# A hybrid decoder layer: SiLU by its own activation, decays computed one supertile ahead, two PSUM banks for the chunk products

## The chip, the cores and the metric

The kernel runs on one core of a Trainium2 chip. The metric is the device time of one execution in microseconds (us). The engines are TensorE (PE in the profile; its weight loads are PEld), VectorE (DVE), ScalarE (ACT), GpSimd (POOL), and the DMA queue that SyncE (SP) issues to.

## The reference

One layer over a prompt of 4096 tokens, 1024 wide, and 8 sample tokens. `h = x * (1 + scale) + shift` is projected by `w_in`. Head group A is a gated delta rule on 4 heads of 128; head group B is attention in a window of 128 with sinks. Both are gated, joined, projected by `w_out` and normalised. What the change touches:

```python
qkv = silu(causal_conv(h @ w_in[:, :1536], conv_w))      # 4 taps per channel
q, k = l2_normalize(qa) * 128**-0.5, l2_normalize(ka)
beta = sigmoid(...)
g = -exp(a_log) * softplus(... + dt_bias)                # decay, per token and head
G = cumsum(g)                                            # within a chunk
dec = exp(G[t] - G[i]) for t >= i
lower = I + beta * (k @ k.T) * dec                       # inverted per chunk
a_qk = (q @ k.T) * dec
```

## The kernel before, in words

The work has three stages. Stage one walks over 16 supertiles of 256 tokens, two chunks of 128 each, and does head group A. Stage two walks over 32 tiles of 128 tokens and does the window attention. Stage three does the gates `z`, the output projection and the normalisation for 16 pairs of tiles. The sample tokens are worked in between as side tasks.

One supertile of stage one goes through `front(s, ...)` (from line 260), `lanes` (line 405), `gdn_inv` (line 440) and `gdn_c` (line 485):

- Lines 262 to 284 project 8 columns of beta and decay (`bd`, from `wbd` and `hT`), and form `be` and `g16`. The softplus is `softplus_ops` (line 96): one `Exp` on ACT (`spu`, line 101) and a polynomial of ten small DVE instructions in a row (lines 103 to 106).
- `group` (line 296) is called for keys, queries and values (blocks 4 to 7, 0 to 3, 8 to 11 of the projection). Each makes two pairs of blocks, 48 matmuls of 128x256 a pair into `pj`; ACT copies (lines 309, 313), DVE adds three taps a block (line 315). Then the gate: ACT's `Tanh` into `th` (line 321) and one DVE instruction `(th + 1) * dst` (line 322), which leaves twice the SiLU.
- Lines 329 to 350 make the decays: the running sum `G` by two matmuls from `g16` (into `tr`), its `Exp` (line 333), and for each chunk a bank `pga` of matmuls, four `Exp` into `dec` (line 348) and one into `eGl` (line 349).
- Lines 352 to 359 transpose the keys of a chunk into `tr`; ACT squares them and scales them with `dec` to `Kd`.
- Lines 370 to 382 make the products keys by keys and keys by queries in bank `pga`, two heads at a time; DVE turns them into `U` and `Aqk`. `lanes` starts the inverse of `U` with 62 small DVE instructions (lines 421, 423) between trips through DRAM.

PSUM has eight banks here: `pga` 1, `xt` 1 (side tasks), `tr` 1 (transposes), `pj` 2, `pgi` 3.

The order on each engine is not that of the source. The framework's scheduler puts the instructions of all engines in order ahead of time, by its own costs and by program order as priority, and fills gaps on TensorE with projection matmuls of a neighbouring supertile. Each engine then works its list strictly in that order and waits where an operand is late.

`dec_b1` (line 914) is the sample tokens' attention; it loads keys, values and sinks for 8 samples with 24 transfers. `loadS` (line 1008) fetches the 7 MB weights `wz` and `wo` of stage three, each in one transfer.

Of the kernel before, what the change touches and what calls it, by code (L numbers as in the profile page):

```python
# [9 lines left out]
F32 = mybir.dt.float32  # L10
F16 = mybir.dt.float16
# [6 lines left out]
D = 1024  # L18
OFF_AZ = 1536
# [14 lines left out]
def body(ctx, tc, I, O, seq):  # L34
# [76 lines left out]
    with ExitStack() as p1:  # L111
# [7 lines left out]
        pga = p1.enter_context(tc.tile_pool(name="pga", bufs=1, space=PSUM))  # L119
        pxt = p1.enter_context(tc.tile_pool(name="pxt", bufs=1, space=PSUM))  # L120
# [139 lines left out]
        def front(s, hT, ahead):  # L260
# [11 lines left out]
            be = sml.tile([128, 2, 4], F32, name="be")  # L272
# [8 lines left out]
            g16 = sml.tile([128, 2, 8], F16, name="g16")  # L281
            gf = g.rearrange("p a b -> p (a b)")
            dve.tensor_copy(g16[:, 0], gf)
            dve.tensor_sub(g16[:, 1], gf, g16[:, 0])
            kqv = wk.tile([128, 8, 256], F32, name="kqv", bufs=2)
# [7 lines left out]
            sc = sml.tile([128, 6, 8], F32, name="sc")  # L293
# [35 lines left out]
            ps = tr_ps([128, 8])  # L329
            mm(ps, triU, g16[:, 0], True, False)  # L330
            mm(ps, triU, g16[:, 1], False, True)
            G = sml.tile([128, 4, 8], F32, name="G")
            act.activation(G[:, 0], ps, AF.Exp)
            act.activation(G[:, 1], ps, AF.Copy, scale=-1.0)
            dve.tensor_scalar(G[:, 2], G[:, 0], -1.0, None, op0=ALU.mult)
            eGl = sml.tile([128, 2, 4], F32, name="eGl")
            decs = []
            for c in range(2):
                dec = wf.tile([128, 4, 128], F32, name="dec", bufs=2)
                pg = pga.tile([128, 4, 128], F32, name="pga")  # L340
                for h in range(4):
                    m = 4 * c + h
                    mm(pg[:, h, :], idb, negm, True, False)
                    mm(pg[:, h, :], g16[:, 0, m:m + 1].to_broadcast([128, 128]), triU, False, False)
                    mm(pg[:, h, :], g16[:, 1, m:m + 1].to_broadcast([128, 128]), triU, False, True)
                for h in range(4):
                    m = 4 * c + h
                    act.activation(dec[:, h, :], pg[:, h, :], AF.Exp, bias=G[:, 1, m:m + 1])
                act.activation(eGl[:, c, :], pg[:, :, 127], AF.Exp)
                decs.append(dec)  # L350

# [8 lines left out]
            dve.tensor_scalar(sse[:, 1], sse[:, 1], 4e-6, None, op0=ALU.add)  # L360
            dve.tensor_scalar(sc[:, 5], sse[:, 1], 0.25, None, op0=ALU.mult)
            pool.tensor_tensor(sc[:, 0], sc[:, 5], half_pos[:, 0:8], op=ALU.pow)
# [30 lines left out]
            dve.tensor_scalar(sc[:, 4], sse[:, 0], 4e-6, 1.28e-4, op0=ALU.add, op1=ALU.mult)  # L393
# [307 lines left out]
        load_bd()  # L701
        for g in (4, 5, 6, 7):
            split_w1(g, wst[g - 4])
# [5 lines left out]
        def ahead(s):  # L709
            if s < NS:  # L710
                nxt[0] = xt(s, load_x(s))

        for s in range(NS):
            kqv, G, sc, U16, Aqk, Kd, Vn, eGl, vt, vt16 = front(s, nxt[0], lambda: ahead(s + 1))
# [25 lines left out]
    with ExitStack() as p2:  # L740
# [173 lines left out]
        def dec_b1(T):  # L914
            sp.dma_start(O["swa_k_s"][0, :, 0:127], I["cache_swa_k"][0, :, 1:128])
            sp.dma_start(O["swa_v_s"][0, :, 0:127], I["cache_swa_v"][0, :, 1:128])
            ps = tr_ps([128, 6, 16])
# [43 lines left out]
            Vc = T.tile([128, 8, 128], F32, name="eVc")  # L961
            for b in range(8):
                kT = T.tile([128, 129], F32, name="ekT", bufs=2)
                sp.dma_start(kT[:, 0:128], I["ckT"][b])
                sp.dma_start(Vc[:, b, :], I["cache_swa_v"][0, b].rearrange("t a d -> t (a d)"))
                dve.tensor_copy(kT[:, 128:129], kn[:, b:b + 1])
                mm(ps_s, Qz[:, b * 64:(b + 1) * 64], kT, b == 0, b == 7)
            sk = T.tile([64, 1], F32, name="esk")
            for b in range(8):
                sp.dma_start(sk[8 * b:8 * b + 8, :], I["sinks"].rearrange("o h -> h o"))  # L970
# [37 lines left out]
        def loadS(w, blk):  # L1008
            sp.dma_start(w.rearrange("p r q a k c -> p r (q a k c)"), wS[blk].rearrange("r p x -> p r x"))
# [278 lines left out]
        for i in range(NT):  # L1288
# [7 lines left out]
            if i == 2:  # L1296
                loadS(wz, 0)
# [22 lines left out]
        loadS(wo, 1)  # L1320
# [74 lines left out]
def layouts(a):  # L1395
# [9 lines left out]
    def chan(v):  # L1405
# [23 lines left out]
        "ckT": a["cache_swa_k"][0].reshape(8, 128, 128).transpose(0, 2, 1),  # L1429
# [27 lines left out]
```

## Time and profile before

| | us |
|---|---|
| median of 3 runs (2236.66 to 2239.43) | 2238.08 |
| the profiled execution | 2235.32 |
| its span, first to last instruction | 2233.5 |
| TensorE busy in the span | 2098.6 (94%) |
| VectorE busy | 1831.9 (82%) |
| ScalarE busy | 1269.1 (57%) |
| mean granted TensorE clock, share of full speed | 0.982 |

The profile is of one execution; line numbers are those of the kernel above. "Busy" is the time that an engine spends on instructions. A wait is idle time of an engine just before an instruction, put down to the event that came last before it started. Stage one ends at about 1100 us, stage two at about 1570 us.

### The profile page before, as it was taken

How to read it: one execution, taken by the hardware profiler on the slowest of the kernel's cores; microseconds unless marked ns; L12 is line 12 of the kernel's file. 1: busy time of each engine (PE TensorE's matmuls, PEld its weight loads, DVE VectorE, ACT ScalarE, POOL GpSimd, SP SyncE). 2: the span in 40 equal slices, each digit the busy share in tenths (PEclk: the TensorE clock that was granted, in tenths of full speed). 3: DMA queues.
4: the chain of work that ended last, by engine and by line, in shares of the span. 5: the costliest groups of instructions: out<-in, count | busy, mean ns of one | idle time of the engine just before them, and what ended most of it. 6: DMA issues, size and time to landing. Idle time of an engine off the chain costs nothing.

```text
span 2233.5 us, 48900 instructions
## 1 busy us (share of the span) xinstructions
PE 2098.6 (94%) x18287; PEld 1497.6 (67%) x18287; DVE 1831.9 (82%) x5546; ACT 1269.1 (57%) x3601; POOL 163.4 (7%) x284
## 2 busy tenths in 40 slices
PE   6989999999989999898999999999999999999997
PEld 4877888878778888777676777776445545444443
DVE  7778889888889989888878977776786787888877
ACT  6666877666767776655446666666443333334332
POOL 1101111111111111011000000000000000000000
PEclk9999999999999999999999999999998999999999
DMA  8333332332233332213153111110532333323222
GB/s 331 105 114 92 130 91 93 119 105 68 88 98 107 107 115 81 67 51 114 54 215 119 59 60 60 61 58 23 222 100 91 131 114 114 117 87 132 95 98 72
DMA packets 141679, 232.21 MB, mean 104 GB/s; under 512 B 62852, under 2 KB 75448, under 8 KB 135272
## 3 DMA queue, kind: packets, MB, share of 16 engines
q1 hardware_dynamic: 140144, 228.53, 30.1%
q8 instruction: 144, 2.36, 0.4%
q14 instruction: 95, 0.78, 0.1%
q10 hardware_dynamic: 1296, 0.55, 0.1%
HBM read 154.07 MB, written 76.09 MB: 103 GB/s over the span
## 4 chain that ended last, share of the span: by engine, by line
PE 53%; DVE 28%; ACT 11%; DMA 4%; issue 3%; POOL 0%; POOLq 0%; SPq 0%; ACTq 0%; DVEq 0%
PE pp L1042 21%; PE pj L41 11%; PE pgi L41 6%; DVE kqv L315 5%; DVE lt L421 3%; PE pga L41 3%; ACT Sm L872 3%; DVE LV L423 3%; PE po L41 2%; PE tr L41 2%; PE tr L889 2%; DMA x<-in_xT_dram 1%; DVE kqv L322 1%; PE xt L41 1%; PE pS L41 1%
## 5 line engine op out<-in xcount | busy, mean ns | idle before, releaser
L41 PE MATMUL pj<-hT,w 128*128 128x256 f16 x4608 | 575.7, 275 | 3.4 <-ACT hT L255 2.6
L41 PEld LDWEIGHTS <-w 128*128 128x128 f16 x4800 | 450.0, 99 | 65.1 <-issue 11.4
L1042 PEld LDWEIGHTS <-S 128*128 128x128 f16 x1536 | 150.6, 99 | 171.4 <-issue 5.0
L41 PEld LDWEIGHTS <-hT 128*128 128x128 f16 x2048 | 159.8, 98 | 68.8 <-issue 4.1
L41 PE MATMUL pj<-wq,hT 128*128 128x512 f16 x768 | 194.8, 379 | 1.1 <-DVE qt L783 0.6
L315 DVE SCALAR_TENSOR_TENSOR kqv<-u,cols,kqv 128x256 f32<-128x256 f32 x384 | 181.9, 480 | 3.7 <-ACT kqv L313 3.1
L1042 PE MATMUL pp<-wz,S 128*128 128x512 f16 x768 | 182.1, 383 | 0.0
L1042 PE MATMUL pp<-wo,S 128*128 128x512 f16 x768 | 171.3, 379 | 0.7 <-DVE zs L1218 0.6
L872 ACT ACTIVATE Sm<-Sm,nm 128x256 f32<-128x256 f32 (+1 forms) x256 | 125.5, 492 | 56.0 <-DVE nm L869 56.0
L1042 PE MATMUL pp<-wz,hT 128*128 128x512 f16 x576 | 131.9, 380 | 1.2 <-ACT zs L1129 1.2
L421 DVE TENSOR_TENSOR lt<-LV,LU 128x60 f32<-128x60 f32 (+24 forms) x496 | 120.2, 242 | 5.8
L1042 PE MATMUL pp<-wo,A 128*128 128x512 f16 x540 | 122.1, 379 | 0.0
L865 DVE CUSTOM_DVE_ANT_0 Sm<-pS,swam 128x256 f32<-128x256 f32 (+1 forms) x256 | 96.2, 415 | 28.2 <-PE tr L889 27.3
L423 DVE TENSOR_TENSOR LV<-LV,lt 128x60 f32<-128x60 f32 (+24 forms) x496 | 103.4, 208 | 5.8
L1042 PEld LDWEIGHTS <-hT 128*128 128x128 f16 x612 | 59.8, 98 | 71.8 <-issue 2.8
L41 PE MATMUL pj<-wkv,hT 128*128 128x256 f16 x768 | 105.6, 273 | 0.0
L1081 POOL TENSOR_TENSOR rs<-rs,cf 128x1 f32<-128x1 f32 (+1 forms) x33 | 22.8, 692 | 1070.7 <-DVE rs L1080 1070.7
L41 PE MATMUL pga<-kqv 128*128 128x256 f32 x256 | 72.2, 401 | 24.2 <-DVE kqv L322 24.1
L1042 PEld LDWEIGHTS <-A 128*128 128x128 f16 x540 | 52.8, 99 | 62.0
L1023 ACT ACTIVATE S<-zt 128x512 f16<-128x512 f32 x64 | 40.3, 630 | 85.7 <-DVE zt L1029 81.4
L1136 ACT ACTIVATE zs<-zs 128x512 f32<-128x512 f32 x48 | 30.2, 629 | 101.3 <-DVE zs L1135 101.2
L315 DVE SCALAR_TENSOR_TENSOR vv<-u,cols,vv 128x256 f32<-128x256 f32 x192 | 82.3, 479 | 1.7 <-ACT vv L313 1.0
(378 smaller groups left out, 4574.7 us busy)
## 6 DMA issues: line engine op xcount, KB each, us to landing
hT<-hD SPq DMA_DIRECT2D x32, 1024.0 KB
x<-in_xT_dram SPq DMA_DIRECT2D x32, 512.0 KB
hD<-hT SPq DMA_DIRECT2D x16, 1024.0 KB
x<-in_x_prompt_dram SPq DMA_DIRECT2D x60, 256.0 KB
out_y_prompt_dram<-x SPq DMA_DIRECT2D x60, 256.0 KB
stg<-in_ws_dram SPq DMA_DIRECT2D x16, 512.0 KB
LU<-D SPq DMA_DIRECT2D x64, 128.0 KB
wS<-wt SPq DMA_DIRECT2D x16, 512.0 KB
```

The lines of the kernel that those rows point to most:

```text
L41: pe.matmul(out, l, r, start=st, stop=sp_)
L315: dve.scalar_tensor_tensor(d, u[:, b2, j:j + 256], cwj(j, blk), d, op0=ALU.mult, op1=ALU.add)
L322: dve.scalar_tensor_tensor(dst, th, 1.0, dst, op0=ALU.add, op1=ALU.mult)
L421: dve.tensor_mul(lt[:, j0:, 0:j], LV[:, j0:, j:j + 1].to_broadcast([128, n, j]), LU[:, None, 0:j, j].to_broadcast([128, n, j]))
L423: dve.tensor_add(LV[:, j0:, 0:j], LV[:, j0:, 0:j], lt[:, j0:, 0:j])
L865: dve.tensor_tensor_reduce(Sm[:, h, k0:256], pS[:, h2, k0:256], swam[:, k0:256], 0.125, -1e30, op0=ALU.add, op1=ALU.max, accum_out=mx[:, h ...
L872: act.activation(Sm[:, h, k0:256], Sm[:, h, k0:256], AF.Exp, bias=nm[:, h:h + 1], accum_out=sm_[:, h:h + 1])
L889: pe.transpose(pt[:, h2, kb, :], Sm[:, h + h2, kb * 128:(kb + 1) * 128], ident)
L1023: act.activation(q[:, 0], src, AF.Copy)
L1042: pe.matmul(dst.rearrange("p (u c) -> p u c", c=128), A[:, hi, k, :], W[:, k // 2::2, q, wi, k % 2, :], start=new and n == 0, stop=n == 11 ...
L1081: pool.tensor_tensor(rs[0:n, 1:2], rs[0:n, 0:1], half_neg[0:n, 0:1], op=ALU.pow)
L1136: act.activation(zs, zs, AF.Silu, scale=IWS)
```

## The change

1. `group` ends with one ACT instruction `Silu` in place; the `Tanh` and the DVE instruction of line 322 go, and with them the factor two (4e-6 becomes 1e-6, and one small DVE instruction before the power goes).
2. The lines on beta, decay, `G`, `dec` and `eGl` become a function `decays(hT)`. It is called once before the loop and then at the end of each `front`, for the next supertile. Its small results get 3 buffers, `dec` 4.
3. `add_manual_dep` edges keep an order on ACT: each `Silu` behind the last exponential issued, each exponential of `decays` behind the last `Silu`. They carry no semaphore.
4. `pga` gets two banks; the side tasks' bank `xt` goes, and they share `tr`.
5. The sample attention's 24 loads become 3, at its start. `wz` is loaded in eight pieces, one a tile of stage two from the third on; `wo` in eight pieces in a row.

```diff
-        pga = p1.enter_context(tc.tile_pool(name="pga", bufs=1, space=PSUM))
-        pxt = p1.enter_context(tc.tile_pool(name="pxt", bufs=1, space=PSUM))
+        pga = p1.enter_context(tc.tile_pool(name="pga", bufs=2, space=PSUM))
...
         def xt_ps(shape, dt=F32):
-            return pxt.tile(shape, dt, name="xt")
+            return pst.tile(shape, dt, name="tr")
...
+        def after_exps(i):
+            if "exp" in order:
+                tc.add_manual_dep(i.ins, order["exp"].name, NOSYNC, reason="gates after exponentials")
+            order["gate"] = i.ins
+        def after_gates(i):
+            if "gate" in order:
+                tc.add_manual_dep(i.ins, order["gate"].name, NOSYNC, reason="exponentials after gates")
+            order["exp"] = i.ins
+        def decays(hT):
...
+            ps = tr_ps([128, 8])
+            mm(ps, triU, g16[:, 0], True, False)
+            mm(ps, triU, g16[:, 1], False, True)
+            G = sml.tile([128, 4, 8], F32, name="G", bufs=3)
+            after_gates(act.activation(G[:, 0], ps, AF.Exp))
...
+                for h in range(4):
+                    m = 4 * c + h
+                    after_gates(act.activation(dec[:, h, :], pg[:, h, :], AF.Exp, bias=G[:, 1, m:m + 1]))
+                after_gates(act.activation(eGl[:, c, :], pg[:, :, 127], AF.Exp))
...
-                th = wf.tile([128, 4, 256], F32, name="th", bufs=1)
-                act.activation(th, dst, AF.Tanh, scale=0.5)
-                dve.scalar_tensor_tensor(dst, th, 1.0, dst, op0=ALU.add, op1=ALU.mult)
+                after_exps(act.activation(dst, dst, AF.Silu))
...
+            if s + 1 < NS:
+                nxt.append(decays(nxt[0]))
             return kqv, G, sc, U16, Aqk, Kd, Vn, eGl, vt, vt16
...
-        def loadS(w, blk):
-            sp.dma_start(w.rearrange("p r q a k c -> p r (q a k c)"), wS[blk].rearrange("r p x -> p r x"))
+        def loadS(w, blk, r):
+            sp.dma_start(w[:, r].rearrange("p q a k c -> p (q a k c)"), wS[blk, r])
...
-            if i == 2:
-                loadS(wz, 0)
+            for r in range(8):
+                if i == min(2 + r, NT - 3):
+                    loadS(wz, 0, r)
```

How the order moves, in the eleventh supertile. First ACT between the keys' gate and the decays, as it was before (`kqv<-pj` is a convolution's start, `th` the gate's Tanh, `Kd` the scaled keys):

```order
L309 ACTIVATE u<-pj 128x2x256
L313 ACTIVATE kqv<-pj,cw_77 128x256 x2
L321 ACTIVATE th<-kqv 128x1024
L333 ACTIVATE G<-tr 128x8
L334 ACTIVATE G<-tr 128x8
L348 ACTIVATE dec<-pga,G 128x128 x4
L349 ACTIVATE eGl<-pga 128x4
L358 ACTIVATE junk,sse<-tr 128x128
L359 ACTIVATE Kd<-tr,dec 128x128
```

The same place on ACT in the changed kernel (`stg` is a side task, L360 the Silu of the keys):

```order
L302 ACTIVATE G<-tr 128x8
L303 ACTIVATE G<-tr 128x8
L317 ACTIVATE dec<-pga,G 128x128 x4
L318 ACTIVATE eGl<-pga 128x4
L317 ACTIVATE dec<-pga,G 128x128 x4
L318 ACTIVATE eGl<-pga 128x4
L694 ACTIVATE stg<-stg,deg 128x128 x4
L360 ACT_TABLE_LOAD
L360 ACTIVATE kqv<-kqv 128x1024
```

The keys' gate stood ahead of the decays' exponentials and now stands behind all of them and behind a table load. A second load stands ahead of the next supertile's softplus, on ACT (`be` is beta's Tanh, `spu` the softplus' Exp):

```order
L286 ACTIVATE be<-x_10400 128x8
L253 ACTIVATE x<-x,shiftT,scaleT 128x256 x3
L535 ACTIVATE r,ss<-oq 128x128 x4
L102 ACT_TABLE_LOAD
L102 ACTIVATE spu<-spab 128x8
```

The kernel before has no load at these two places; it has 4 loads in all, and the changed kernel 38. On DVE, before, from the last steps of the inverse to the first reads of the queries' products (`kqv<-th,kqv` is the queries' gate, `vv` the values' convolution, `LV` and `lt` steps of the inverse):

```order
L423 TENSOR_TENSOR LV<-LV,lt 128x8x2
L421 TENSOR_TENSOR lt<-LV,LU 128x8
L322 SCALAR_TENSOR_TENSOR kqv<-th,kqv 128x1024
L423 TENSOR_TENSOR LV<-LV,lt 128x8
L315 SCALAR_TENSOR_TENSOR vv<-u,cols,vv 128x256 x6
L379 SCALAR_TENSOR_TENSOR U<-pga,sc,dec 128x128 x2
L382 TENSOR_TENSOR Aqk<-pga,dec 128x256
```

The same place on DVE in the changed kernel:

```order
L355 SCALAR_TENSOR_TENSOR vv<-u,cols,vv 128x256 x2
L393 SCALAR_TENSOR_TENSOR U<-pga,sc,dec 128x128
L355 SCALAR_TENSOR_TENSOR vv<-u,cols,vv 128x256
L469 TENSOR_TENSOR XZ<-pgi,XZ 64x4x64
L355 SCALAR_TENSOR_TENSOR vv<-u,cols,vv 128x256
L393 SCALAR_TENSOR_TENSOR U<-pga,sc,dec 128x128
L396 TENSOR_TENSOR Aqk<-pga,dec 128x256
```

The gate's instruction is gone from the list; in its place the first reads of the products (`U`) stand between the values' convolutions, one head at a time.

## Rows read from the trace of the kernel before

**Rows 1.** The page: busy time of each engine, share of the span, instructions.
```profile
PE 2098.6 (94%) x18287; PEld 1497.6 (67%) x18287; DVE 1831.9 (82%) x5546; ACT 1269.1 (57%) x3601; POOL 163.4 (7%) x284
```

**Rows 2.** Busy time by stretch: length, each engine's busy us, granted clock, DMA.
```profile
230.00:1010.00 780.00, 729.65 (x7350) 632.16 (x7347) 692.21 (x2417) 541.44 (x1740) 103.38 (x184) 0.99 0.29 93
1010.00:1110.00 100.00, 87.54 (x770) 68.89 (x769) 83.05 (x305) 49.67 (x170) 7.26 (x12) 0.95 0.28 87
1110.00:1540.00 430.00, 421.88 (x4731) 306.56 (x4729) 330.65 (x1242) 263.70 (x808) 2.01 (x2) 1.00 0.23 84
```

**Rows 3.** Waits of PE, whole span: waiter, releaser, us in total, times, longest.
```profile
PE pga L41 <- DVE kqv L322: 24.1, 16, 2.3
PE tr L41 <- DVE g L283: 11.3, 9, 2.8
PE tr L355 <- DVE kqv L322: 4.0, 5, 1.0
PE pga L41 <- ACT eGl L349: 1.3, 2, 0.8
PE tr L399 <- DVE vv L322: 1.2, 1, 1.2
```

**Rows 4.** Groups of instructions: count, busy us, mean ns, idle before.
```profile
L322 DVE SCALAR_TENSOR_TENSOR kqv<-th,kqv 128x1024 f32<-128x1024 f32 x32 | 39.1, 1221 | 8.6 <-ACT th L321 8.6
L321 ACT ACTIVATE th<-kqv 128x1024 f32<-128x1024 f32 x32 | 34.0, 1062 | 57.0 <-DVE kqv L315 57.0
L348 ACT ACTIVATE dec<-pga,G 128x128 f32<-128x128 f32 x128 | 37.2, 387 | 6.7 <-PE pga L41 6.4
L1136 ACT ACT_TABLE_LOAD x2 | 2.6, 1283 | 0.0
```

**Rows 5.** ACT in order of time at one table load: start, length.
```profile
1567.28 0.63 ACT L1023 ACTIVATE S<-zt 128x512 f16<-128x512 f32 x1 [3.13 <-PE pp L1042]
1567.92 1.28 ACT L872 ACT_TABLE_LOAD   x1
1569.22 0.51 ACT L872 ACTIVATE Sm<-Sm,nm 128x256 f32<-128x256 f32 x1
```

**Rows 6.** PE in order of time, before one queries' product.
```profile
714.22 0.66 PE L355 MATMUL tr<-cf,kqv 128*128 128x128 f32 x4 [0.26 <-ACT Kd L359]
714.72 6.28 PE L41 MATMUL pj<-hT,w 128*128 128x256 f16 x56
722.27 1.13 PE L41 MATMUL pga<-kqv 128*128 128x256 f32 x4 [1.28 <-DVE kqv L322]
```

**Rows 7.** ACT in the same stretch: the queries' Tanh.
```profile
719.69 1.06 ACT L321 ACTIVATE th<-kqv 128x1024 f32<-128x1024 f32 x1 [2.17 <-DVE kqv L315]
```

**Rows 8.** DVE in the same stretch: the queries' gate.
```profile
721.00 1.22 DVE L322 SCALAR_TENSOR_TENSOR kqv<-th,kqv 128x1024 f32<-128x1024 f32 x1
```

**Rows 9.** DVE in order of time along one softplus.
```profile
696.11 0.17 DVE L103 TENSOR_SCALAR spp<-spu 128x8 f32<-128x8 f32 x1
...
703.38 0.27 DVE L421 TENSOR_TENSOR lt<-LV,LU 128x60 f32<-128x60 f32 x1
703.55 0.17 DVE L105 SCALAR_TENSOR_TENSOR spp<-spp,spu 128x8 f32<-128x8 f32 x1
703.63 0.49 DVE L315 SCALAR_TENSOR_TENSOR kqv<-u,cols,kqv 128x256 f32<-128x256 f32 x1
704.02 0.22 DVE L423 TENSOR_TENSOR LV<-LV,lt 128x60 f32<-128x60 f32 x1
...
708.09 0.17 DVE L283 CAST g<-g 128x8 f16<-128x8 f32 x1
...
717.14 0.24 DVE L421 TENSOR_TENSOR lt<-LV,LU 128x49 f32<-128x49 f32 x1
717.30 0.16 DVE L360 TENSOR_SCALAR sse<-sse 128x8 f32<-128x8 f32 x1
717.42 0.21 DVE L423 TENSOR_TENSOR LV<-LV,lt 128x49 f32<-128x49 f32 x1
```

More of the change, by code (lines that the diff above doesn't have):

```diff
@@ L18 @@
 D = 1024
+NOSYNC = mybir.DependencyInfo(mybir.DependencyClass.NoSync, mybir.DependencyReason.DATA)
 OFF_AZ = 1536
@@ L258, in xt @@
             return hT
-        def front(s, hT, ahead):
+        order = {}
+        def after_exps(i):
[7 more added lines that the diff above has]
+        def decays(hT):
             bd = tr_ps([128, 2, 16])
@@ L271, in front @@
             dve.tensor_add(x8, bdS[:, :, 0:8], bdS[:, :, 8:16])
-            be = sml.tile([128, 2, 4], F32, name="be")
+            be = sml.tile([128, 2, 4], F32, name="be", bufs=3)
             act.activation(be, x8[:, :, 0:4], AF.Tanh, scale=0.5)
@@ L280, in front @@
             dve.tensor_scalar(g, g, -30000.0, None, op0=ALU.max)
-            g16 = sml.tile([128, 2, 8], F16, name="g16")
+            g16 = sml.tile([128, 2, 8], F16, name="g16", bufs=3)
             gf = g.rearrange("p a b -> p (a b)")
@@ L284, in front @@
             dve.tensor_sub(g16[:, 1], gf, g16[:, 0])
+            ps = tr_ps([128, 8])
[3 more added lines that the diff above has]
+            after_gates(act.activation(G[:, 0], ps, AF.Exp))
+            act.activation(G[:, 1], ps, AF.Copy, scale=-1.0)
+            dve.tensor_scalar(G[:, 2], G[:, 0], -1.0, None, op0=ALU.mult)
+            eGl = sml.tile([128, 2, 4], F32, name="eGl", bufs=3)
+            decs = []
+            for c in range(2):
+                dec = wf.tile([128, 4, 128], F32, name="dec", bufs=4)
+                pg = pga.tile([128, 4, 128], F32, name="pga")
+                for h in range(4):
+                    m = 4 * c + h
+                    mm(pg[:, h, :], idb, negm, True, False)
+                    mm(pg[:, h, :], g16[:, 0, m:m + 1].to_broadcast([128, 128]), triU, False, False)
+                    mm(pg[:, h, :], g16[:, 1, m:m + 1].to_broadcast([128, 128]), triU, False, True)
+                for h in range(4):
+                    m = 4 * c + h
+                    after_gates(act.activation(dec[:, h, :], pg[:, h, :], AF.Exp, bias=G[:, 1, m:m + 1]))
+                after_gates(act.activation(eGl[:, c, :], pg[:, :, 127], AF.Exp))
+                decs.append(dec)
+            return be, g16, G, eGl, decs
+        def front(s, hT, dcy, ahead):
+            be, g16, G, eGl, decs = dcy
             kqv = wk.tile([128, 8, 256], F32, name="kqv", bufs=2)
@@ L292, in front @@
             sse = sml.tile([128, 2, 8], F32, name="sse")
-            sc = sml.tile([128, 6, 8], F32, name="sc")
+            sc = sml.tile([128, 5, 8], F32, name="sc")
             junk = wf.tile([128, 128], F32, name="junk", bufs=1)
@@ L328, in front @@
             next(qrs)
[L329 to L350, printed above, removed]
             for c in range(2):
@@ L701, in body @@
         load_bd()
+        nxt.append(decays(nxt[0]))
         for g in (4, 5, 6, 7):
@@ L710, in ahead @@
             if s < NS:
-                nxt[0] = xt(s, load_x(s))
+                nxt[:] = [xt(s, load_x(s))]
         for s in range(NS):
-            kqv, G, sc, U16, Aqk, Kd, Vn, eGl, vt, vt16 = front(s, nxt[0], lambda: ahead(s + 1))
+            kqv, G, sc, U16, Aqk, Kd, Vn, eGl, vt, vt16 = front(s, *nxt, lambda: ahead(s + 1))
             Vs = [gdn_inv(c, U16, vt, vt16) for c in range(2)]
@@ L916, in dec_b1 @@
             sp.dma_start(O["swa_v_s"][0, :, 0:127], I["cache_swa_v"][0, :, 1:128])
+            kTs = T.tile([128, 8, 129], F32, name="ekT")
+            sp.dma_start(kTs[:, :, 0:128], I["ckT"])
+            Vc = T.tile([128, 8, 128], F32, name="eVc")
+            sp.dma_start(Vc, I["cvT"])
+            sk = T.tile([64, 1], F32, name="esk")
+            sp.dma_start(sk, I["sink64"])
             ps = tr_ps([128, 6, 16])
@@ L960, in dec_b1 @@
             ps_s = pso.tile([64, 129], F32, name="po")
-            Vc = T.tile([128, 8, 128], F32, name="eVc")
+            dve.tensor_copy(kTs[:, :, 128:129], kn[:, :, None])
             for b in range(8):
[L963 to L970, printed above, removed]
+                mm(ps_s, Qz[:, b * 64:(b + 1) * 64], kTs[:, b], b == 0, b == 7)
             P = T.tile([64, 129], F32, name="eP")
@@ L1319, in body @@
         wo = wop.tile([128, 8, 7, 2, 2, 128], F16, name="wo")
-        loadS(wo, 1)
+        for r in range(8):
+            loadS(wo, 1, r)
         s2 = p2.enter_context(tc.tile_pool(name="s2", bufs=1, **W2))
@@ L1428, in layouts @@
         "scT": a["state_conv"][0].reshape(8, 3, 12, 128).transpose(3, 2, 0, 1),
-        "ckT": a["cache_swa_k"][0].reshape(8, 128, 128).transpose(0, 2, 1),
+        "ckT": a["cache_swa_k"][0].reshape(8, 128, 128).transpose(2, 0, 1),
+        "cvT": a["cache_swa_v"][0].reshape(8, 128, 128).transpose(1, 0, 2),
+        "sink64": np.tile(a["sinks"].reshape(8, 1), (8, 1)),
     }
```

8 lines of the change are left out of this document (4 added, 4 removed).

## The prediction

> **What bounds the kernel now.** I read the page first. TensorE is busy for 94% of the span [rows 1], and in a run of 56 projection matmuls it gives one every 6.28 / 56 = 0.112 us [rows 6]. The reader is to see there that the span is made of TensorE's work, and that no edit of the change takes away or adds a matmul of weight. What can be won is TensorE's idle time and nothing else, so the next view is busy time by stretch. Idle TensorE is 780 - 729.7 = 50.3 us in the steady part of stage one, 12.5 us where stage one passes into stage two, and 430 - 421.9 = 8.1 us in nearly all of stage two [rows 2]. The loads of part 5 belong to stage two, so they can't win more than a small part of 8.1 us. VectorE is busy for 692 of those 780 us, ScalarE for 541 [rows 2]: both have room, VectorE little.
>
> The waits of TensorE say whose lateness that idle time is [rows 3]. The line of the gate (L322) stands there three times: 24.1 us in 16 waits before the products of keys and queries, one in each supertile, 4.0 us before the keys' transposes and 1.2 us before the values'. The softplus chain, whose last link is the cast of `g`, makes 11.3 us, and the bank `pga` still in use by `eGl` 1.3 us. These five rows hold 41.9 us. They are all that the change aims at.
>
> **The gate, 48 of them.** Removed: 48 DVE instructions of 1.221 us [rows 4], 58.6 us of VectorE. ACT's `Silu` in place of `Tanh` has the same 1024 columns, so I give it the Tanh's 1.06 us [rows 4]. VectorE is not the bound, so the 58.6 us as such win nothing; the path does. In the stretch shown the queries' Tanh ran from 719.69 to 720.75 [rows 7], the gate from 721.00 to 722.22 [rows 8], and TensorE's product began at 722.27 after a wait of 1.28 us [rows 6]. Without the gate the product could begin at 720.8: 1.5 us earlier, which is all of that wait. The mean wait is 24.1 / 16 = 1.5 us, so the most to be won is 24.1 us. But the scheduler knows that the chain got shorter. In the order of the kernel before, 64 projection matmuls on average stand between the queries' last projection and the first product; in the changed order 60, and in five of the last ten supertiles 52 or fewer. So 4.5 x 0.112 = 0.5 us of cover is gone too. The mean wait goes from 1.5 to 0.5 us: **-16 us**. Bounds: 0 if the waits form again in full, -24 if they go. The values' gate shortens in the same way: -1 us.
>
> **The keys' gate and the table loads.** It loses the same DVE instruction (4.0 us of waits), but ACT now comes to it only after both chunks' exponentials and a table load. The load took 1.28 us, and from the end of the instruction ahead of it (1567.91) to the start of the one behind it 1.31 us went by [rows 5]. There are 34 more loads, 44 us of ACT, and ACT has 239 idle us in the steady part alone [rows 2], so ACT as a whole holds. Whether the load is on the path is a matter of cover. After the last decay matmul ACT needs at most 8 exponentials of 37.2 / 128 = 0.29 us [rows 4], a load of 1.31 and a Silu of 1.06: 4.7 us. In the changed order 36 to 46 projections stand there in most of the supertiles, 4.0 to 5.2 us, with side tasks' matmuls between them, and 26 or 27 in the last three, which is 3 us. The first chunk's exponentials run while the second's matmuls do, so the need is nearer 4 us. I take 3 us of waits in all in place of the 4.0: **-1 us**. Bounds: -4, and +16 x 1.31 = +21 if every load is late in full.
>
> The Trainium skill, "ScalarE: Activation LUTs", section "What ACT_TABLE_LOAD costs", puts a switch at 1283 ns for the load and 1380 ns of drain, 2.66 us. Only the first part agrees with this trace (1.28 us); no drain is seen in rows 5. By the page the 34 loads would take 90 us of ACT, and the upper bound of this part would be +43 us instead of +21.
>
> **The softplus chain.** It is started one `front` ahead, so by program order it comes before the next supertile's work, and the scheduler packs it closer: in the order before 92 projections stand between `bd` and the first matmul that reads `g16` (mean from the fourth supertile on), in the changed order 71, that is 8.0 us, 8.5 with the other matmuls. Against it stands a chain of 15 small DVE instructions with steps of the inverse between them and, in the order I looked at, six convolutions. A link with a step of the inverse takes 717.42 - 717.14 = 0.28 us, one with a convolution as well 704.02 - 703.38 = 0.64 us [rows 9]: 9 x 0.28 + 6 x 0.64 = 6.4 us. Ahead of it come the copy of `bd`, two sums, beta's Tanh, a table load (1.31) and an Exp, 2.0 to 3.0 us. That makes 8.4 to 9.4 us against 8.5 us of cover: a mean wait near 0.9 us where it was 11.3 / 16 = 0.7. I take 14 us for the 11.3: **+3 us**. Bounds: -11, if the chain is always covered; from above the pace of the old chain, which took 708.1 - 696.1 = 12.0 us over the same links with far more work between them [rows 9]: with 3 us ahead of it 15 us, 6.5 us a supertile too long. I take the value near the lower rows, since the work that stretched the old chain (updates of the state, side tasks) stands elsewhere in the new order.
>
> **Two banks for `pga`, one for `tr` and `xt`.** The wait for `eGl` goes, -1 us. The products of four pairs of heads can follow each other; that hastens DVE's `U`, not TensorE. In exchange a side task's matmul (sample state, gate factors) and the keys' transposes now share a bank, and the keys wait for DVE to have read it. The projections between them cover this in the plan; +1 us, bounds 0 and +1.3 x 16 = +21 (the longest such hold would be two reads of half a gate's length).
>
> **Loads.** Part 5 costs and wins nothing: in stage two no wait for a transfer is among TensorE's, and all idle time there is 8 us [rows 2]. If the cover of eight smaller pieces fails, the price is at most that again.
>
> **Sum.** -16 - 1 - 1 + 3 - 1 + 1 = -15 us. Against the profiled execution, 2235.3 us, that is 2220.3. The median of the three runs shown lies 2.8 us above that execution, so the forecast for a median is **2223 us**. With the parts' likely spread (the queries' gate -24 to -8, the softplus chain -8 to +10) its own range is 2207 to 2237.
>
> **Rivals.** (A) The waits form again: the scheduler moves each product forward by what the chain lost, and TensorE arrives as much too early as before. For it speaks that cover did shrink in the changed order; against it that it shrank by 0.5 us and the chain by 1.5. Half the gain (-8) and the softplus chain at +8 give 2238. Chance 0.17.
>
> (B) Slower: the decay chain becomes what TensorE waits for. It has two table loads in it and stands ahead of the keys' gate, so a late `g` delays everything behind it on ACT. If the wait for `g` grows to 2 us in each of 16 supertiles (+21) and half of the keys' loads come late (+11), with -16, -4 and -1 kept for the gates, the sum is +11: 2249 us. It decides over the forecast once the chain takes more than 10 us. For it: the cover was cut from 92 to 71 projections. Against it: old waits for `g` were short in spite of VectorE's 89% there, and VectorE loses 3.7 us a supertile. The drain that the Trainium skill's page "ScalarE: Activation LUTs" adds would make this one worse, 2249 + 22. Chance 0.19.
>
> (C) All 41.9 us go, since VectorE with less to do is on time everywhere: 2196 us. Chance 0.06. (D) That the change does nothing at all is excluded by the order, which has the loads and lacks the gate.
>
> **How the numbers follow.** The forecast has 0.58. The range 2204 to 2249 holds the forecast's own, A and the nearer half of B; what is left out is the far half of B, most of C and a little of the forecast, 0.15. A measurement of this kernel can tell 0.2%, 4.5 us, from no change. Faster by more than that: nearly all of the forecast, and C, 0.62. Within it: A and the forecast's upper end, 0.19. Slower by more: B, 0.19.
>
> **What would show it.** Right: no wait of more than about 10 us in total of the products on the queries' Silu (it was 24.1 on the gate); 34 more loads of 1.28 us; waits for `g` near 14 us; VectorE's busy time down by 55 to 60 us; stage two unchanged. Wrong: waits for `g` above 30 us, or keys' transposes that wait 1 us or more for ACT in each supertile (B); a product that waits 1.5 us for the Silu as it did for the gate (A); a lower granted clock in stage one.

## The result and the profile after

The changed kernel takes **2256.04 us** (median of 6 runs, 2246.24 to 2258.91) against 2237.43 for the kernel before (6 runs): a ratio of 1.0078, 95% interval 1.0063 to 1.0094. It is slower by some 17 us by the ratio, where 15 fewer were forecast, and it lies above the range. Five of its six executions took 2253 to 2259 us at a mean granted clock of 0.974 to 0.977, the sixth 2246 at 0.982. The profiled execution took 2253.03 us with a span of 2251.2. Its page has this first line, beside [rows 1]:

```profile
PE 2106.4 (94%) x18287; PEld 1504.0 (67%) x18287; DVE 1789.7 (79%) x5475; ACT 1308.3 (58%) x3635; POOL 149.2 (7%) x284
```

The same 18287 matmuls. VectorE has 42 us less to do, ScalarE 39 more. TensorE is busy for 7.8 us more with the same work and idle for 9.9 us more (2251.2 - 2106.4 = 144.8 against 2233.5 - 2098.6 = 134.9), which together is the 17.7 us between the spans.

To see where, cut both spans where the two kernels have issued about the same number of matmuls (to within 50). First the kernel before, busy time by stretch; the columns are those of [rows 2] (length, then busy us and count of PE, PEld, DVE, ACT, POOL, then the granted clock, the DMA share, GB/s):

```profile
0.00:150.00 150.00, 125.93 (x1171) 98.51 (x1172) 116.69 (x318) 102.80 (x253) 17.63 (x39) 0.94 0.52 187
150.00:320.00 170.00, 155.50 (x1559) 134.24 (x1557) 141.73 (x494) 116.64 (x362) 23.80 (x35) 0.96 0.36 113
320.00:1050.00 730.00, 679.19 (x6765) 587.47 (x6762) 645.39 (x2249) 493.71 (x1609) 95.09 (x173) 0.99 0.29 92
1050.00:1250.00 200.00, 189.36 (x1981) 137.89 (x1982) 161.66 (x592) 110.92 (x348) 4.03 (x4) 0.97 0.35 124
1250.00:2233.50 983.50, 948.60 (x6820) 539.49 (x6817) 766.41 (x1896) 445.00 (x1035) 22.83 (x33) 0.99 0.27 95
```

and the changed kernel:

```profile
0.00:152.00 152.00, 125.59 (x1164) 97.92 (x1165) 107.81 (x308) 110.06 (x261) 18.85 (x39) 0.93 0.48 175
152.00:336.00 184.00, 159.25 (x1554) 138.66 (x1553) 138.51 (x503) 121.81 (x366) 19.06 (x36) 0.92 0.32 100
336.00:1060.00 724.00, 682.30 (x6815) 590.33 (x6813) 617.93 (x2188) 521.69 (x1632) 84.60 (x171) 0.99 0.31 95
1060.00:1268.00 208.00, 191.09 (x1947) 138.38 (x1945) 158.84 (x581) 112.27 (x347) 4.21 (x5) 0.97 0.33 120
1268.00:2251.20 983.20, 948.20 (x6819) 538.73 (x6816) 766.57 (x1898) 442.51 (x1032) 22.45 (x33) 0.99 0.27 95
```

The steady part of stage one, on which the forecast mainly rested, is 6 us faster (730 to 724), with 50.8 - 41.7 = 9 us less idle. The stretch ahead of it, in which the pipeline of supertiles fills, is 14 us slower (170 to 184), the passage into stage two 8 us (200 to 208), the start 2 us. (Cut at exactly equal numbers of matmuls, as in the table of stretches below, the steady part gains 11 us and the passage loses 11.) From there on to the end the two take the same, 983.5 and 983.2 us. The granted clock fell with it in the filling stretch, from 0.96 to 0.92, one of the forecast's signs of being wrong.

TensorE's waits over the whole span, with the columns of [rows 3]; these are the lines that answer to that group:

```profile
PE tr L42 <- DVE g L296: 23.7, 15, 2.5
PE pga L42 <- ACT kqv L360: 7.0, 8, 2.5
...
PE tr L370 <- ACT kqv L360: 1.3, 3, 0.5
...
PE tr L413 <- ACT vv L360: 0.9, 2, 0.7
```

The queries' gate went from 24.1 to 7.0 us, the keys' from 4.0 to 1.3, the values' from 1.2 to 0.9; the wait for `g` doubled, from 11.3 to 23.7; a wait for `eGl` is no longer among them. The five waits of [rows 3] held 41.9 us, what answers to them 32.9.

What happens in the filling stretch is seen in the projections `pj` alone, in slices of 10 us (length, PE busy and count, clock, DMA share, GB/s). The kernel before:

```profile
160.00:170.00 10.00, 0.00 (x0) 0.79 0.45 158
170.00:180.00 10.00, 0.00 (x0) 0.66 0.23 80
180.00:190.00 10.00, 2.19 (x19) 1.00 0.50 147
```

and the changed one:

```profile
160.00:170.00 10.00, 0.00 (x0) 0.74 0.76 245
170.00:180.00 10.00, 0.00 (x0) 0.50 0.37 123
180.00:190.00 10.00, 0.00 (x0) 0.74 0.00 0
190.00:200.00 10.00, 4.81 (x45) 1.00 0.39 134
```

In both kernels the first inverse and the first update of the state run bare, without a projection between their steps, until the third supertile's projections go on in the order. In the kernel before no projection starts from 155 to 186 us, in the changed one from 156 to 195, and the granted clock falls to 0.50 in the middle of it. The inverse starts later because `lanes` ends later: its result leaves by DMA at 149.0 us, before at 144.1.

`lanes` is VectorE's. VectorE's waits between 95 and 150 us, the kernel before (the sample tokens' projection `us` in the side tasks' own bank):

```profile
DVE us L588 <- ACT ul L587: 2.3, 1, 2.3
```

the changed kernel:

```profile
DVE us L604 <- ACT ul L603: 8.3, 1, 8.3
DVE gateT L174 <- PE tr L42: 2.5, 1, 2.5
```

and VectorE there in order of time (start, length; `LV` and `lt` are the first steps of the first inverse):

```profile
106.34 0.23 DVE L174 TENSOR_SCALAR gateT<-tr,cols 128x9 f32<-128x9 f32 x1 [2.50 <-PE tr L42]
114.91 0.26 DVE L604 SCALAR_TENSOR_TENSOR us<-tr,ul 128x96 f32<-128x96 f32 x1 [8.34 <-ACT ul L603]
...
119.56 0.21 DVE L437 TENSOR_TENSOR lt<-LV,LU 128x31 f32<-128x31 f32 x1
```

VectorE, which works its list in order, stands still behind `us` for 8.3 us with the inverse's first step queued behind it. What it waits for is on TensorE: the 192 small matmuls of `us`, which now stand in bank `tr` (the bracket: 2.75 us idle, waiting for nothing that the profile shows),

```profile
106.62 4.54 PE L42 MATMUL tr<-hsT,w 128*128 128x16 f16 x172
113.92 0.67 PE L42 MATMUL tr<-hsT,w 128*128 128x8 f16 x20 [2.75 <-issue]
```

and stood in a bank of their own before, in two runs with transposes of the values between:

```profile
90.88 3.43 PE L41 MATMUL xt<-hsT,w 128*128 128x16 f16 x130
94.16 0.63 PE L399 MATMUL tr<-cf,vv 128*128 128x128 f32 x4
94.63 1.73 PE L41 MATMUL xt<-hsT,w 128*128 128x16 f16 x62
```

So `tr` is held from 106.6 to 114.9 us, and the side task comes some 16 us later than before. The inverse's first step on VectorE starts at 117.1 us before and at 119.6 here, 2.5 us later. That this late first inverse is what makes the changed kernel slow is not shown, and three of the runs below speak against it. decays_only, with the old PSUM and only 2.3 us of the wait for `us`, hands over at 149.8 us and has no projection from 158 to 198; in xt_in_pga the gap lasts from 153 to 192, in cns_own from 159 to 201; and these take 2241, 2238 and 2239 us.

### The profile page after: what moved, and what is told of

Same layout as the page of the kernel before. It is cut to its first block, busy times and chain, and to the rows that moved or that the text cites. A ratio compares the mean times of both kernels' runs of the same rounds, so it can differ in the third digit from the quotient of the medians.

```text
span 2251.2 us, 48797 instructions
## 1 busy us (share of the span) xinstructions
PE 2106.4 (94%) x18287; PEld 1504.0 (67%) x18287; DVE 1789.7 (79%) x5475; ACT 1308.3 (58%) x3635; POOL 149.2 (7%) x284
## 4 chain that ended last, share of the span: by engine, by line
PE 57%; DVE 23%; ACT 12%; issue 3%; DMA 3%; POOL 0%; SPq 0%; POOLq 0%; ACTq 0%; DVEq 0%
PE pp L1058 21%; PE pj L42 13%; PE pgi L42 7%; DVE kqv L355 4%; PE tr L42 3%; DVE lt L437 3%; PE pga L42 3%; ACT Sm L889 3%; DVE LV L439 2%; PE po L42 2%; PE tr L906 2%; PE pS L42 1%; DVE vv L355 1%; DVE bst L1093 1%; ACT junk L406 1%
## 5 line engine op out<-in xcount | busy, mean ns | idle before, releaser
L1058 PEld LDWEIGHTS <-S 128*128 128x128 f16 x1536 | 150.6, 99 | 171.5 <-issue 5.0
L42 PEld LDWEIGHTS <-PT 128*128 128x128 f16 x1512 | 60.7, 100 | 35.6 <-ACT PT L909 21.2
```

The costliest lines, as they stand in the source:

```text
L42: pe.matmul(out, l, r, start=st, stop=sp_)
L1058: pe.matmul(dst.rearrange("p (u c) -> p u c", c=128), A[:, hi, k, :], W[:, k // 2::2, q, wi, k % 2, :], start=new and n == 0, stop=n == 11 ...
```

## The experiments

Three parts of the change can be had or not: the new PSUM (part 4), the decays one supertile ahead with their order edges (parts 2 and 3), and Silu (part 1). The runs fill all eight cells. Ratios are to the kernel before on the same chip, with the 95% interval; the rows with decays ahead have the loads in pieces too.

| PSUM | decays | gate | run | median us | ratio |
|---|---|---|---|---|---|
| as before | in place | Tanh | the kernel before | 2234 to 2237 | 1 |
| as before | in place | Silu | silu_only | 2219.58 | 0.9932 [0.9915, 0.9949] |
| as before | ahead | Tanh | decays_only | 2241.00 | 1.0030 [1.0019, 1.0041] |
| as before | ahead | Silu | psum_back | 2230.45 | 0.9973 [0.9961, 0.9985] |
| new | in place | Tanh | psum_only | 2249.70 | 1.0062 [1.0041, 1.0082] |
| new | in place | Silu | silu_psum | 2246.02 | 1.0042 [1.0028, 1.0057] |
| new | ahead | Tanh | old_gate | 2253.16 | 1.0077 [1.0048, 1.0106] |
| new | ahead | Silu | the changed kernel | 2256.04 | 1.0078 [1.0063, 1.0094] |

Their profiled executions by stretch, in us, each cut where TensorE has started its 1171st, 2730th, 9495th and 11476th matmul; the last three rows are runs told of below, all on the changed kernel. It is one execution each: that of silu_psum lies 6 us above its median, that of old_gate 6 below.

| run | start | filling | steady | passage | rest |
|---|---|---|---|---|---|
| the kernel before | 150.0 | 170.4 | 730.8 | 200.1 | 982.3 |
| silu_only | 147.1 | 171.3 | 701.3 | 214.3 | 982.1 |
| decays_only | 152.7 | 181.0 | 724.1 | 199.6 | 981.7 |
| psum_back | 146.1 | 177.8 | 714.4 | 208.6 | 982.7 |
| psum_only | 152.9 | 175.5 | 722.1 | 213.2 | 984.5 |
| silu_psum | 154.3 | 176.9 | 723.6 | 213.5 | 982.0 |
| old_gate | 152.5 | 178.8 | 722.1 | 210.0 | 981.9 |
| the changed kernel | 152.6 | 184.9 | 720.0 | 210.7 | 983.0 |
| share_only | 150.6 | 182.2 | 735.4 | 217.0 | 983.2 |
| xt_in_pga | 150.1 | 181.3 | 712.6 | 205.0 | 985.1 |
| cns_own | 156.1 | 181.2 | 712.5 | 204.1 | 982.0 |

Read in pairs, the decays ahead lengthen the filling stretch in all four, by 3 to 11 us, and shorten the passage, by 1 to 6. The PSUM's price falls on other stretches in each pair: with neither of the other parts on the passage (13 us, and the steady part gains 9), beside the Silu on the steady part (22), beside the decays ahead on the passage again (10), beside both on the start, the filling and the steady part (6 to 7 each).

**The PSUM undone, the PSUM alone.**

```diff
-        pga = p1.enter_context(tc.tile_pool(name="pga", bufs=2, space=PSUM))
+        pga = p1.enter_context(tc.tile_pool(name="pga", bufs=1, space=PSUM))
+        pxt = p1.enter_context(tc.tile_pool(name="pxt", bufs=1, space=PSUM))
...
-            return pst.tile(shape, dt, name="tr")
+            return pxt.tile(shape, dt, name="xt")
```

> The changed kernel with its PSUM as before: one bank for the chunk products, the side tasks' own bank again. Theory S (the side tasks and the transposes now share one bank; in the first four supertiles the sample convolution gets late by 40 us, its two output transfers stand ahead of the fourth supertile's input on SyncE's queue, and TensorE is left with bare inverses at half clock): the 22 us that the changed kernel has lost by 315 us come back, the later lag of stage two stays: 2230 to 2240 us, sample convolution out near 219 us. Theory D (the decays and the Silu's table loads cost more than they win): at most 3 us change, 2252 to 2259 us.

Measured 2230.45: theory S is borne out in its numbers. `lanes` hands over its result at 136.6 us, against 149.0 in the changed kernel. The kernel is now faster than before, yet by 6 us only: by the table of stretches the start and the steady part gain 4 and 16 us on the kernel before, the filling and the passage lose 7 and 9. TensorE's waits in it:

```profile
PE pga L42 <- ACT kqv L361: 19.9, 15, 2.3
PE tr L42 <- DVE g L297: 11.6, 13, 1.7
...
PE tr L371 <- ACT kqv L361: 4.5, 14, 0.5
```

With the old PSUM the queries' wait has formed again, behind the Silu: 19.9 us where it was 24.1 behind the gate. That is rival A. The other way round, the kernel before with lines 1 and 2 of the PSUM changed and nothing else:

> The kernel before with nothing but the new PSUM: two banks for the chunk products, side tasks in the transposes' bank. Theory S: slower by 8 to 22 us, 2245 to 2260 us. Theory D: within 4 us of before, 2233 to 2242 us.

Measured 2249.70, as theory S had it. Its waits:

```profile
PE tr L41 <- DVE g L282: 23.8, 15, 2.6
...
PE pga L41 <- DVE kqv L321: 4.6, 7, 1.1
```

So the exchange of 20 us of queries' wait for 12 us of wait for `g` comes with the PSUM and not with the Silu: it is there with the old gate in its old place. It needs neither of the other parts, but it does not always come: in old_gate, with the new PSUM, the two waits are 13.5 and 11.3 us.

**Which half of the PSUM.** First, one bank for the products again while the side tasks stay in `tr` and the eighth bank is empty:

```diff
-        pga = p1.enter_context(tc.tile_pool(name="pga", bufs=2, space=PSUM))
+        pga = p1.enter_context(tc.tile_pool(name="pga", bufs=1, space=PSUM))
```

> The changed kernel with one bank for the chunk products; the side tasks still share the transposes' bank, and the eighth bank stays empty. If sharing the bank is the cost: 2246 to 2258 us, like the changed kernel. If it is the second bank for the products, by the order that it brings: 2226 to 2236 us, like the run with the old PSUM (2230.5).

2270.83 (ratio 1.0163, 1.0142 to 1.0185), above both ranges: 42 us over psum_back by the ratios, for nothing but the side tasks' move into `tr`. The cost is with the sharing, and the second bank for the products gives a part of it back, 19 us. By the table of stretches half of the 42, 21 us, lies in the steady part. Then the side tasks in the two product banks instead of the transposes':

```diff
         def xt_ps(shape, dt=F32):
-            return pst.tile(shape, dt, name="tr")
+            return pga.tile(shape, dt, name="pga")
```

> The changed kernel with the side tasks in the two banks of the chunk products instead of the transposes' bank. If sharing with the transposes and the decays' sums is what costs: 2228 to 2238 us, like the old PSUM (2230.5). If a bank less for the side tasks costs wherever it is taken from: 2246 to 2260 us.

2238.12 (ratio 1.0013, 1.0002 to 1.0024): 14 us less than the changed kernel by the ratios, by the choice of partner and the order that follows from it. The wait for `g` is still 23.8 us in it, so that doubled wait is not what makes the changed kernel slow. `lanes` hands over at 147.4 us, little earlier than in the changed kernel, so the first inverse is not what is won here; the larger part is won in the steady stretch and in the passage into stage two (7 and 6 us in the table).

**A theory that fell: the blocked input.** The sample convolution's output takes two of the three buffers `x` through which the supertiles' input comes, and in the changed kernel it leaves 43 us later than before (262 against 219).

```diff
-            cns = [wf.tile([8, 1024], F32, name="x", bufs=3) for _ in range(2)]
+            cns = [wf.tile([8, 1024], F32, name="cns", bufs=2) for _ in range(2)]
```

> The changed kernel with two buffers of their own for the sample convolution's output, which took two of the three input buffers x. Theory X (the fourth supertile's input waits behind that output, for the buffers and in the queue, and that is most of the 22 us): the lag at 315 us falls to 10 us or less and the time to 2236 to 2246 us. Theory Y (the shared bank delays the inverse, the products and g themselves; the input is late only on paper): 2250 to 2258 us.

2239.22 (ratio 1.0028, 1.0013 to 1.0043): the time lies where theory X put it, but the lag does not. The filling stretch is as late as ever:

```profile
0.00:155.00 155.00, 126.90 (x1161) 98.69 (x1162) 107.97 (x308) 110.33 (x262) 20.30 (x39) 0.92 0.49 175
155.00:336.00 181.00, 161.00 (x1562) 139.69 (x1561) 139.71 (x510) 122.81 (x367) 19.62 (x36) 0.92 0.31 99
```

336 us, as in the changed kernel. The gain, 11 us by the ratios, came later, in the steady part and in the passage. By its own mark theory X is wrong. Two buffers for a side task moved so much so far away: such an edit gives the scheduler another order, and a step of 5 us between two such kernels says little of its edit, one of 11 us not much. What speaks for the PSUM as a cause is that it costs in all four pairs of the table, 10 to 25 us. The same edit on top of psum_back:

> The changed kernel with the PSUM as before and the sample convolution's output in buffers of its own. The PSUM alone gave 2230.5, the buffers alone 2239.2. If the output still held the input x in the old PSUM, some us more are won: 2222 to 2228 us. If with the old PSUM it was out in time (219 us, as in the kernel before), nothing more: 2228 to 2234 us.

2234.58 (ratio 0.9996, 0.9985 to 1.0008): no gain, and 5 us worse than psum_back by the ratios.

**The gate.** The changed kernel with Tanh and VectorE's instruction back (and the factor two, as in the kernel before):

```diff
-                after_exps(act.activation(dst, dst, AF.Silu))
+                th = wf.tile([128, 4, 256], F32, name="th", bufs=1)
+                act.activation(th, dst, AF.Tanh, scale=0.5)
+                dve.scalar_tensor_tensor(dst, th, 1.0, dst, op0=ALU.add, op1=ALU.mult)
```

> The changed kernel with the old gate (Tanh, then VectorE's instruction), so without the 34 table loads; decays ahead, order edges and PSUM stay. Theory S: the early loss stays and VectorE's 58 us come back: 2254 to 2268 us. Theory D with the table loads as the cost: back to 2236 to 2246 us, waits for g under 15 us.

2253.16, just under theory S's range: no better and no worse than with Silu. Under the new PSUM the Silu is worth nothing that can be told (0 us with the decays ahead, 4 with them in place, both within the intervals). Under the old one it is. The same edit on top of psum_back, so with the decays ahead:

> The PSUM as before, decays ahead and the loads in pieces, but the old gate (no table loads). The same with Silu took 2230.5. If Silu wins what is won (VectorE's 58 us, the queries' gate): 2233 to 2240 us. If the decays ahead win it and Silu gives its gain back in table loads and order edges: 2224 to 2232 us.

2241.00: 13 us slower than psum_back by the ratios, which has the Silu, and 7 slower than the kernel before. So the decays ahead (with their order edges) do not pay here: they cost, and the Silu wins it back. Then the Silu by itself, in the kernel before:

```diff
-                th = wf.tile([128, 4, 256], F32, name="th", bufs=1)
-                act.activation(th, dst, AF.Tanh, scale=0.5)
-                dve.scalar_tensor_tensor(dst, th, 1.0, dst, op0=ALU.add, op1=ALU.mult)
+                act.activation(dst, dst, AF.Silu)
```

> The kernel before with Silu for its gate and nothing else: decays in their old place, 64 more table loads. If the gate's gain holds against twice the loads: 2222 to 2231 us. If the loads (64 x 1.28 us, 82 us of ScalarE) come on the path between the keys' gate and the decays: 2236 to 2255 us.

2219.58, below the lower range: 15 us faster than before, in spite of 68 table loads where the changed kernel has 38. The queries' wait falls by less than that, from 24.1 to 13.6 us, and the wait for `g` stays at 11.2; by stretches the steady part gains 29 us and the passage loses 14. And silu_only with the PSUM's edit of psum_only:

> The kernel before with Silu and the new PSUM, decays in their old place. Silu alone gave 2219.6 (16 less than before), the PSUM alone 2249.7 (14 more). If the two add: 2230 to 2238 us. If the PSUM costs more where the decays are ahead, the changed kernel's loss needs all three, and this one stays under 2230; if it costs as much as in the changed kernel (26): 2242 to 2250 us.

2246.02: neither of the simple sums. By the ratios the PSUM costs 14 us beside the old gate and 25 beside the Silu where the decays are in place, 10 and 23 where they are ahead.

**The price of the table loads.** In the changed kernel they look like this, groups of ACT by line and then one load in order of time:

```profile
L360 ACT ACTIVATE kqv<-kqv 128x1024 f32<-128x1024 f32 x32 | 34.1, 1065 | 14.5 <-DVE kqv L355 14.4
L360 ACT ACT_TABLE_LOAD x17 | 21.8, 1283 | 0.3
L102 ACT ACT_TABLE_LOAD x16 | 20.5, 1283 | 0.3
```

```profile
719.21 1.33 ACT L694 ACTIVATE stg<-stg,deg 128x128 f32<-128x128 f32 x4
720.57 1.28 ACT L360 ACT_TABLE_LOAD   x1
721.86 1.06 ACT L360 ACTIVATE kqv<-kqv 128x1024 f32<-128x1024 f32 x1
```

The Silu takes the Tanh's time (1065 and 1062 ns), and from the end of one instruction to the start of the next across a load 721.86 - 720.54 = 1.32 us go by. The run without them, on top of psum_back:

```diff
-                after_exps(act.activation(dst, dst, AF.Silu))
+                after_exps(act.activation(dst, dst, AF.Tanh))
```

> The PSUM as before, and Tanh in the place of Silu, of the same shape: it computes another gate and leaves the product with its input out, and needs 4 table loads in place of 36. It is the price of the loads alone, against 2230.5 with Silu. If they are hidden in ScalarE's idle time: 2226 to 2232 us. If one load in each of 16 supertiles stands on the path (16 x 1.31 us): 2208 to 2216 us.

2227.51 (ratio 0.9966, 0.9953 to 0.9978) against 0.9973 with the 32 loads: 1.6 us, inside both intervals. What the loads cost by themselves cannot be told more sharply, since the order on TensorE differs between the two runs from the 330th matmul on; but 16 loads in full on the path are ruled out.

**The loads in pieces**, undone in the changed kernel (the sample attention's too):

```diff
-            for r in range(8):
-                if i == min(2 + r, NT - 3):
-                    loadS(wz, 0, r)
+            if i == 2:
+                loadS(wz, 0)
...
-        for r in range(8):
-            loadS(wo, 1, r)
+        loadS(wo, 1)
```

> The changed kernel with the loads of the sample attention and of the large weights as before. If the loads are what makes stage two start 7 us later than stage one ends late (the lag grows from 11 to 18 us between 1140 and 1240 us): 2247 to 2251 us. Theories S and D alike, with the loads costing nothing: 2253 to 2259 us.

2257.65 (ratio 1.0086, 1.0063 to 1.0109): nothing, in either direction.

**More cover for `g`.** psum_back with the call of `decays` moved ahead of the values' first blocks:

```diff
             next(qrs, None)
+            if s + 1 < NS:
+                nxt.append(decays(nxt[0]))
             next(vls)
...
-            if s + 1 < NS:
-                nxt.append(decays(nxt[0]))
```

> The PSUM as before and Silu, with the decays of the next supertile called before the values' first blocks instead of at the end of front. In the plan 94 projections stand between bd and the first matmul that reads g, as against 87. If the waits for g (8.8 us between 300 and 1050 us with the old PSUM) go and no other comes: 2220 to 2227 us. If the waits for the queries' Silu (14.9 us there) grow in their place: 2228 to 2236 us.

2273.41 (ratio 1.0181, 1.0154 to 1.0209), a miss of both: 46 us more than psum_back by the ratios, although the order has more projections between `bd` and `g`'s first reader. The wait grew all the same:

```profile
PE tr L42 <- DVE g L297: 28.9, 15, 3.1
```

**More cover for the queries.** psum_back with all of the values' projections ahead of the products:

```diff
             next(qrs, None)
             next(vls)
+            next(vls, None)
...
-            next(vls, None)
             for c in range(2):
                 pv = tr_ps([128, 4, 128])
```

> The PSUM as before, Silu, and all of the values' projections before the products of keys and queries. If the waits for the queries' Silu (14.9 us between 300 and 1050 us) go and nothing takes their place: 2213 to 2222 us. If the inverse, which starts later, or g then ends last: 2230 to 2245 us.

2216.16 (ratio 0.9915, 0.9898 to 0.9932): 13 us less than psum_back by the ratios. The same edit on top of silu_only, without decays ahead and without the new PSUM:

> The kernel before with Silu, and all of the values' projections before the products. Silu alone gave 2219.6 and still has 12.5 us of waits for the queries' Silu between 320 and 1050 us. If the later products take them away as they did with the decays ahead (2216.2 against 2230.5, 14 us): 2205 to 2212 us. If VectorE, with the inverse still behind it, then sets the pace: 2214 to 2222 us.

**2210.50** (ratio 0.9883, 0.9868 to 0.9898), 26 us faster than the kernel before and 44 us faster than the changed one by the ratios: the version that beats both. Its steady part, for about the same matmuls as the 730 us of before, and then its waits for `g` and for the queries, whole span:

```profile
311.00:1011.00 700.00, 675.14 (x6784) 589.95 (x6782) 627.47 (x2222) 550.59 (x1671) 82.34 (x172) 0.99 0.31 99
```

```profile
PE tr L41 <- DVE g L283: 2.2, 2, 1.2
...
PE pga L41 <- ACT kqv L320: 0.7, 1, 0.7
```

24.1 and 11.3 us of waits have become 0.7 and 2.2. The same move with the old gate:

> The kernel before with its own gate, and all of the values' projections before the products. If what Silu won was only the wait of the products (24.1 us in the kernel before), the cover alone wins it too: 2212 to 2222 us. If VectorE's 58.6 us for the gate count as well: 2226 to 2240 us.

2265.14 (ratio 1.0127, 1.0109 to 1.0144), above both ranges and 28 us slower than before. VectorE is now what the products wait for:

```profile
PE pga L41 <- DVE Aqk L383: 13.4, 10, 2.0
...
PE tr L355 <- DVE kqv L322: 10.7, 13, 0.9
```

The same move wins 11 us beside the Silu and loses 28 beside the old gate. So the 58.6 us of VectorE, which I said win nothing as such, are by these waits what lets a later product be afforded.

## Why the prediction was wrong

**Right.** The table loads cost nothing that can be measured: 34 more, of 1.28 us each. The price of 1380 ns of drain that the Trainium skill gives in "ScalarE: Activation LUTs", section "What ACT_TABLE_LOAD costs", is not seen here either: 1.32 us pass from end to start. Loads in pieces: nothing, as forecast. `eGl`'s wait went, 1.3 us.

**Met by luck.** The queries' wait fell by 17.1 us in the changed kernel (forecast 16), the values' by 0.3 (1), the keys' by 2.7 (1). But the large fall is not the shorter gate's: with the new PSUM and the old gate (psum_only) the queries' wait is 4.6 us, and with the Silu and the old PSUM (psum_back) it is 19.9. There it formed again, as rival A had it. The Silu alone wins 15 us by its ratio, where the forecast's gate terms make 18, yet only 10.5 us of queries' wait went, where 16 were forecast; to which waits the rest of its gain belongs is not shown.

**The step that failed: "Two banks for `pga`, one for `tr` and `xt`", -1 and +1 us, with a bound of +21.** Measured, by the ratios: 14 us alone and 25 beside the Silu with the decays in place, 10 and 23 with them ahead; two of the four lie beyond the bound. I priced it by the longest single hold of a bank, 1.3 us, in each of 16 supertiles, and let the projections between cover it "in the plan". The longest hold was mis-sized: the 192 matmuls of `us` alone hold `tr` for 8.3 us, with VectorE standing still behind them. The cover failed as well: of the 42 us that the sharing costs in share_only, 21 lie in the steady part, where the projections are. And the new PSUM was priced as if all else stayed in its place, while it gives the scheduler another order of everything: psum_only's matmuls leave the order of the kernel before at the 23rd, and the price lies in other stretches in each pair of the table.

**Second, "The softplus chain", +3 us.** The wait for `g` went up by 12.4 us, not 3. From the end of `bd` to the cast of `g` the chain takes 10.0 us on average from the fifth supertile on (8.4 to 9.4 were forecast); with 8.5 us of cover the mean wait of 23.7 / 16 = 1.5 us follows. But the rise did not come with the decays ahead, to which I put it: psum_back has them and waits 11.6 us, psum_only has them in place and waits 23.8. Nor do the projections counted as cover tell the wait: counted as in the forecast they are 117 in psum_only and 94 in early2, with 23.8 and 28.9 us of wait, and 45 in late_prod, with 2.4. Rival B named the late `g` and put its threshold at 10 us and its time at 2249. B's other half, keys' transposes held up by late table loads, did not come (1.3 us). And the runs with 23.8 us of this wait at 2238 and at 2250 us show that it does not set the time by itself; that the measured time lies nearer to B's than to the forecast is luck of B's.

**Third, the decays ahead were given no cost beyond the waits.** They cost 7 and 9 us under the old PSUM, 3 (within the intervals) and 8 under the new. In all four pairs the filling stretch is longer with them: in decays_only, with the side tasks' bank apart, `lanes` hands over at 149.8 us, in silu_only at 134.8. What delays it there I have not settled.

**Sum.** Against the kernel before, by the ratios: Silu -15, decays ahead with it +9, the PSUM on top of both +23, which is the +17 measured. Rival A's mechanism holds in psum_back (19.9 us of queries' wait), B's first half in the changed kernel, and neither makes it slower than before; the PSUM does. (A's own sum, -8 - 1 - 1 + 8 - 1 + 1, gives 2236 and not 2238.)

**Open.** Through which waits the PSUM costs its 10 to 25 us, and why more beside the Silu than beside the old gate, is not settled. xt_in_pga shows that 14 of its 23 us hang on the partner that the side tasks share a bank with. The hold of 8.3 us and the wait behind it are seen, but the first inverse, late by 9 us at 195 us, is as late in runs that take 2238 to 2241 us. How much of each step is the edit's own and how much another order that any edit would have brought cannot be parted with these runs. The passage (1050 to 1250 us) costs most kernels that are early there 7 us or more again, and I have tested no cause for that.

## What to carry to other kernels

Read the start, the filling and the passage besides the steady part: here the change won in the steady part and lost more in the others. Price a shared buffer by the longest chain that will hold it, and not by a typical hold, and ask who is queued behind its reader on an engine that works in order. With a scheduler ahead of time, a shortened chain wins what the order then leaves uncovered; the last gain here, 11 us on top of the Silu's 15, came from moving cover to the chain that still waited, and it needed the engine freed first. Try the parts of a change one by one and in pairs: here one part won 15 us by itself and a later one took all of it and more.

## What was not expected of the hardware

The granted clock does nearly as much as the waits. TensorE did the same 18287 matmuls in 2098.6 us before and 2106.4 after, and in 2123.9 in early2, at mean granted clocks of 0.982, 0.976 and 0.970. In the changed kernel's bare inverse, with no projection between its steps, the clock is 0.74 at 160 to 170 us and at its lower level, 0.50 (1.2 GHz), at 170 to 180; so a gap that opens there is paid for twice.

The 48 VectorE instructions that went sum to 58.6 us, but VectorE's busy time fell by 42 only, where 55 to 60 were forecast. Consecutive records overlap there (one from 119.69 for 0.48 us, the next from 120.08, in the changed kernel) and the overlap counts once; that this makes the whole difference is not shown.
